# A decoder layer's attention: the projections written as one paced stream through DRAM

## The chip, the core and the metric

The kernel runs on one core of a Trainium2 chip. The core's engines work side by side, each on its own list of instructions in a fixed order: TensorE (PE in the profile, with its weight loads listed as PEld), VectorE (DVE), ScalarE (ACT), GpSimd (POOL) and SyncE (SP), which here issues nearly all DMAs. The metric is the device time of one execution in microseconds. Before the change it is 3108.72 us (median of three runs, 3105.47 to 3114.95).

## The reference

One decoder layer on 2048 tokens of width 1024, all in float32. The part that the change touches is the token mixer:

```
h = rms_norm(x, g_attn) * (1 + scale_a) + shift_a        # scale and shift from silu(c) @ w_ada
q_f, k_f, v_f, q_s, k_s, v_s, f_logit = split(h @ w_in)  # 8 + 8 heads of 64 columns
FoX:  s = q.k/8 + F[t] - F[s], causal;  softmax(s) @ v   # F = cumsum(log_sigmoid(f_logit + b))
SB:   z = q.k/8;  a[t,s] = sigmoid(z_ts) * prod_{s<j<t} (1 - sigmoid(z_tj)), s < t;  a @ v
x = x + gate_a * (concat(head_norm(o_fox), head_norm(o_sb)) @ w_out)
```

Behind it come a gated MLP with a short causal convolution (inner width 2752) and a final RMSNorm; the change does not touch them.

## The kernel before, in words

Every float32 product is made from two parts: `split` writes a rounded high part (a copy on ACT) and the remainder as a low part (a subtraction on DVE or POOL), and TensorE multiplies three of the four pairs (high with high, high with low, low with high) at the rate of the rounded type. Q.K takes two matmuls, because Q and K are laid out with high and low parts on 128 partitions.

Attention is cut into 32 units `(kind, p, tb)`: `kind` is `sb` (stick-breaking, first) or `fox`, `p` one of four pairs of heads, `tb` one of four blocks of 512 queries. The list runs over `tb` within `p` within `kind`, and unit 0 is `(sb, 0, 0)`. A unit with `tb` = 3 looks back over four blocks of keys, one with `tb` = 0 over one. Each unit has two bodies of work.

- **Projection** (`proj` and `finish_proj`, L368 and L284; `norm_proj` for the pair `(sb, 0)`, which also makes the normed input and stores it in the DRAM tiles `hs`). Eight input tiles `hp` are loaded from `hs` (10 buffers), 24 matmuls of 512 columns make q and 24 make k (both at L282, into the two PSUM banks `ps_pj`), and every second pair of heads also makes v for itself and the next pair (96 matmuls of 256 columns at L323, 264 for the first pair). q and k are split into tiles `q2` (2 buffers). From there four DMAs each copy them, from SBUF to SBUF, into the tiles `Q` (2 buffers) and `K` (5 buffers) that attention reads. v goes to a tile `V` (6 buffers); the second pair's goes through a tile `V` to the DRAM tile `vs` and is loaded from there later.
- **Attention** (`attend`, L492). A tile of logits is 128 queries by up to 512 keys: two matmuls (L405, L406) into `ps_qk`. For SB, ACT takes two sigmoids (L437, L438) and DVE runs the product as a scan (L443); for FoX, DVE adds the decay and finds the minimum (L472), and ACT takes the exponential (L476). Then TensorE transposes blocks of 128 (L415, into `ps_pt`), ACT and DVE split them into `at` (L419, L420), and TensorE multiplies with V (L424, 256 columns, into `ps_pv`).

The order of all this is set in two steps. In the source, `interleave` (L132) walks through the attention of unit i, and after each of its steps it takes steps of the projection of unit i+1, in proportion: 7, 12 or 19 projection steps over the unit's attention steps; what is left of that projection is written behind the last attention step. From the FoX unit 17 on, the same loop also takes four steps a unit of `late_mod`, which computes later modulation vectors from `w_ada` and folds a gate into `w_out` (its tiles are `hp` tiles too). Then a scheduler moves instructions: each engine gets its list by priority of the source's order, but what is ready sooner, by its own model of the buffers, is taken first. So the projection of unit i+1 is moved forward as far as its buffers let it: `Q` has two buffers, and the copy into the next one waits for the last logits of unit i-1.

A DMA whose buffer is not free yet waits at the head of SP's list, and everything behind it waits too.

## Time and profile before

| | |
|---|---|
| time of the profiled execution | 3105.93 us |
| its span, first to last instruction | 3103.7 us |
| granted TensorE clock, mean | 0.986 |
| startup and unit 0 (to its last product with V) | 105.6 us |
| units 1 to 31 | 105.6 to 1560.2 us |
| output projection, MLP and the rest | 1560.2 to 3103.7 us |
| DMA, mean over the span | 163 GB/s |

The boundaries of units used below are the starts of the last L424 matmul of each: a unit's window then holds its own attention, apart from a few logits of the next unit, and whatever projection work the scheduler put there. In a window's row, `(x771)` is the number of instructions that started in it. Matmuls overlap each other, so the busy time of PE is more than the time that their issue takes.

### The profile page before, as it was taken

Reading aid. Unit: us, or ns where it says so; the run is one execution under the profiler, and the core shown is the slowest. Engines: PE = TensorE matmul, PEld = TensorE weight load, DVE = VectorE, ACT = ScalarE, POOL = GpSimd, SP = SyncE. Lnnn points to the kernel's source line nnn. Section 1 sums busy time; section 2 is a strip of 40 time slices with the busy share of each in tenths; the row PEclk is TensorE's granted clock in tenths of the full one; section 3 lists DMA queues with packets and bytes.
Section 4 is the critical chain, followed back from the end, with each engine's and each line's share of the span. In section 5 each row is a group of like instructions: output and inputs, shape, how many; then the busy total and the mean of one; then the engine's idle time right before and its main releaser. Section 6 shows DMA issues by size and latency. Waiting matters only on the chain.

```text
span 3103.7 us, 45389 instructions
## 1 busy us (share of the span) xinstructions
PE 2955.7 (95%) x15934; PEld 2501.2 (81%) x15934; DVE 2071.3 (67%) x3206; ACT 1681.2 (54%) x3129; POOL 986.7 (32%) x1011
## 2 busy tenths in 40 slices
PE   6889999999999999999998899999899998999998
PEld 5788887878888888888877688888678887888887
DVE  6787777787857765567733687778977776254253
ACT  5676767677766665567634544444544443343332
POOL 1541321213131332341122344444444442332321
PEclk8999999999999999999999999999999999999999
DMA  9647654737264985694467522223222224565562
GB/s 270 225 136 265 194 166 118 250 99 211 73 191 159 318 271 174 191 319 125 138 200 225 190 79 85 82 83 88 85 82 82 82 82 147 183 203 166 184 201 87
DMA packets 301396, 504.85 MB, mean 163 GB/s; under 512 B 29712, under 2 KB 186128, under 8 KB 300144
## 3 DMA queue, kind: packets, MB, share of 16 engines
q1 hardware_dynamic: 289536, 489.32, 50.0%
q10 hardware_dynamic: 11632, 12.63, 1.2%
q8 instruction: 126, 2.06, 0.3%
q14 instruction: 102, 0.84, 0.1%
HBM read 356.81 MB, written 94.71 MB: 145 GB/s over the span
## 4 chain that ended last, share of the span: by engine, by line
PE 21%; DVE 10%; POOL 6%; DMA 6%; issue 5%; ACT 2%; SPq 0%; POOLq 0%; ACTq 0%; DVEq 0%
PE ps_o L984 8%; PE ps_t L984 4%; PE ps_bc L984 4%; DMA wuraw<-in_w_up_dram 3%; DVE wu L45 3%; PE ps_o L653 2%; PE ps_o L834 2%; DVE u L903 2%; POOL ws L822 2%; POOL wuraw L821 2%; POOL ws L820 1%; DVE u L924 1%; DVE u L902 1%; DMA r<-rstd 1%; PE ps_t L834 1%
## 5 line engine op out<-in xcount | busy, mean ns | idle before, releaser
L834 PE MATMUL ps_o<-oa,wu 128*128 128x512 f32 x2088 | 503.6, 392 | 13.1 <-DVE oa L45 6.8
L834 PEld LDWEIGHTS ps_o<-oa,wu 128*128 128x128 f32 x2088 | 390.9, 188 | 104.9 <-DVE oa L45 11.3
L420 DVE TENSOR_TENSOR at<-ps_pt,at 128x512 fp32r<-128x512 f32 (+1 forms) x576 | 362.6, 650 | 96.5 <-ACT at L419 94.5
L282 PE MATMUL ps_pj<-hp,w_qk 128*128 128x512 f32 x1512 | 414.0, 404 | 13.1 <-POOL hp L45 4.6
L443 DVE TENSOR_TENSOR_SCAN a<-r,a 128x512 f32<-128x512 f32 (+2 forms) x320 | 371.7, 1177 | 75.9 <-POOL a L440 41.1
L424 PE MATMUL ps_pv<-at,V 128*128 128x256 f32 x2304 | 397.9, 292 | 20.2 <-ACT at L419 9.4
L419 ACT ACTIVATE at<-ps_pt 128x512 fp32r<-128x512 f32 (+1 forms) x576 | 319.0, 578 | 132.8 <-PE ps_pt L415 106.3
L424 PEld LDWEIGHTS ps_pv<-at,V 128*128 128x128 f32 x2304 | 331.4, 190 | 58.9 <-DVE at L420 20.9
L282 PEld LDWEIGHTS ps_pj<-hp,w_qk 128*128 128x128 f32 x1512 | 274.9, 190 | 68.0 <-POOL hp L45 6.5
L45 DVE TENSOR_TENSOR wd<-wdraw,wd 128x1024 fp32r<-128x1024 f32 x88 | 112.4, 1277 | 261.2 <-ACT wd L44 261.1
L405 PE MATMUL ps_qk<-K,Q 128*128 128x512 f32 (+2 forms) x640 | 262.3, 411 | 10.5 <-ACT a L438 4.9
L984 PE MATMUL ps_o<-wd,g 128*128 128x512 f32 x1040 | 250.6, 390 | 8.8 <-ACT g L44 8.8
L45 POOL TENSOR_TENSOR g<-graw,g 128x512 fp32r<-128x512 f32 x84 | 141.1, 1682 | 326.8 <-ACT g L44 326.1
L834 PE MATMUL ps_t<-ob,wu 128*128 128x512 f32 x984 | 241.5, 390 | 0.0
L323 PE MATMUL ps_pj<-w_v,hp 128*128 128x256 f32 (+1 forms) x1536 | 235.8, 291 | 5.3 <-DVE w_v L45 1.8
L406 PE MATMUL ps_qk<-K,Q 128*128 128x512 f32 (+2 forms) x640 | 236.7, 371 | 0.0
L984 PEld LDWEIGHTS ps_o<-wd,g 128*128 128x128 f32 x1040 | 196.0, 189 | 49.9 <-ACT g L44 9.2
L44 ACT ACTIVATE wu<-wuraw 128x512 fp32r<-128x512 f32 x214 | 133.2, 627 | 186.3 <-PE ps_o L834 116.0
L323 PEld LDWEIGHTS ps_pj<-w_v,hp 128*128 128x128 f32 x1536 | 210.7, 193 | 14.2 <-DVE q L291 2.9
L834 PEld LDWEIGHTS ps_t<-ob,wu 128*128 128x128 f32 x984 | 184.7, 188 | 39.1 <-DVE y L886 0.4
L437 ACT ACTIVATE r<-ps_qk 128x512 f32<-128x512 f32 (+2 forms) x320 | 173.6, 543 | 78.2 <-PE ps_qk L406 75.5
L44 ACT ACTIVATE wd<-wdraw 128x1024 fp32r<-128x1024 f32 x88 | 93.1, 1058 | 206.8 <-PE ps_bc L984 193.0
(222 smaller groups left out, 5491.3 us busy)
## 6 DMA issues: line engine op xcount, KB each, us to landing
hp<-hs SPq DMA_DIRECT2D x224, 512.0 KB
wuraw<-in_w_up_dram SPq DMA_DIRECT2D x84, 512.0 KB
wdraw<-in_w_down_dram SPq DMA_DIRECT2D x84, 512.0 KB
Q<-q SPq DMA_DIRECT2D x128, 256.0 KB
g<-u SPq DMA_DIRECT2D x42, 512.0 KB
graw<-g SPq DMA_DIRECT2D x84, 256.0 KB
hs<-hp SPq DMA_DIRECT2D x32, 512.0 KB
K<-q SPq DMA_DIRECT2D x128, 128.0 KB
```

What stands on the lines that cost most here:

```text
L44: nc.scalar.activation(hi, src, AF.Copy)
L45: (lo_engine or nc.gpsimd).tensor_sub(lo, src, f(hi))
L282: nc.tensor.matmul(acc, w[kt][:, a, n], h[:, bb], start=kt == 0 and i == 0, stop=kt == KT - 1 and i == 2)
L323: nc.tensor.matmul(av[:, t * width:(t + 1) * width], hts[kt][:, a, tok], w[1][kt][:, bb, 0:width], start=kt == 0 and m == 0, stop=kt == KT ...
L405: nc.tensor.matmul(b[:, :cw], Q[:, hl, 0, qcols], K[:, hl, :cw], start=True, stop=False)
L406: nc.tensor.matmul(b[:, :cw], Q[:, hl, 1, qcols], K[:, hl, :cw], start=False, stop=True)
L419: nc.scalar.activation(at[:, 0, lo:], b[:, lo:], AF.Copy)
L420: nc.vector.tensor_sub(at[:, 1, lo:], b[:, lo:], f(at[:, 0, lo:]))
L424: nc.tensor.matmul(o[:, 0:2 * P], V[kt // 4][:, kt % 4, hl, :], rhs, start=first and kk == 0 and w == 0, stop=last and kk == 1 and w == 1)
L443: nc.vector.tensor_tensor_scan(rev, r[:, 0:need][:, ::-1], rev, 0.0 if right[qi] is None else right[qi][:, 0:1], ALU.mult, ALU.add)
L834: nc.tensor.matmul(b, w[:, p, j], o[:, q], start=first and i == 0, stop=last and i == 2, skip_group_check=True)
L984: nc.tensor.matmul(banks[t][n], g[:, a, t * P:(t + 1) * P], w[:, b, n * TB:(n + 1) * TB], start=k == 0 and i == 0, stop=k == NKD - 1 and i ...
```

## The change

Four things are written differently; no arithmetic is added or left out.

1. **The projections of units 1 to 31 are one generator**, `project()`, called `ahead`. It is not tied to the next unit any more. `pace(i)` gives, for each attention step of unit i, how many projection steps are to be written by then: the larger of two lines. The first brings the next unit's projection to its end at 0.8 of this unit's steps. The second, from unit 3 on, spreads all remaining projection steps over units 3 to 29 in proportion to a weight of the units' attention, 10 + 16 tb, times 1.4 for SB.
2. **A bound on how far the scheduler moves them.** From unit 3 on, each projection step is written inside `issue_after(...)`: its TensorE instructions stand behind the second logits matmul that is the thirteenth to last written (`LAG` = 12). That is an order on TensorE's list alone, not a wait.
3. **Q, K and V go through DRAM**, but for the pair `(sb, 0)`, whose Q and K, and whose own V, are copied as before. Otherwise `q2` and `k2` are written to a DRAM tile of their own for each unit, both V's to `vs`, and `load_unit` reads them into `Q`, `K` and `V` when the attention of the unit before is under way. The V's that are to be stored are made in `q2` buffers. `V` has 5 buffers in place of 6.
4. `Fb` (the FoX decay, broadcast) has 10 buffers in place of 8.

```diff
-    def finish_proj(kind, p, tb, aq, w, hts, res, ak=None):
+    def staged():
+        return sl_.tile([P, 2, TB], F32R, name="q2", bufs=2)
+    def load_unit(kind, p, tb, res):
+        if (kind, p) == ("sb", 0):
+            return
+        Q, K, V = unit_tiles()
+        src = qs.pop((kind, p, tb))
+        for h in range(2):
+            rows = slice(h * HD, (h + 1) * HD)
+            for r in range(2):
+                half = slice(r * HD, (r + 1) * HD)
+                nc.sync.dma_start(f(Q[half, h]), src[rows, 0])
+                nc.sync.dma_start(f(K[half, h]), src[rows, 1, r])
+        nc.sync.dma_start(f(V), vs[kind][p][tb])
+        res.append((Q, K, V))
+    def finish_proj(kind, p, tb, aq, w, hts, ak=None):
...
+        if direct:
+            for h in range(2):
+                for r in range(2):
+                    nc.sync.dma_start(f(Q[r * HD:(r + 1) * HD, h]), f(q2[h * HD:(h + 1) * HD]))
+        else:
+            q_ = qs[kind, p, tb] = dram.tile([P, 2, 2, TB], F32, name=f"qk_{kind}{p}_{tb}", bufs=1)
+            nc.sync.dma_start(q_[:, 0], f(q2))
...
-            nc.sync.dma_start(spill, f(V1))
+            for e in range(direct, 2):
+                nc.sync.dma_start(vs[kind][p + e][tb], f(Vs[e]))
...
+    def pace(i):
+        n = attend_steps(units[i])
+        due = sum(proj_steps(u) for u in units[:i + 2])
+        total = sum(proj_steps(u) for u in units)
+        done = sum(weight(u) for u in units[START:i])
+        span = sum(weight(u) for u in units[START:STOP])
+        base = sum(proj_steps(u) for u in units[:START + 1])
+        first = projected[0]
+        for m in range(1, n + 1):
+            yield max(first + (due - first) * min(1.0, m / (0.8 * n)),
+                      base + (total - base) * (done + weight(units[i]) * m / n) / span if i >= START else 0)
+    LAG = 12
+    LATE, PER = 17, 4
+    START, STOP = 3, 30
...
+        def follow(m):
+            while projected[0] < goals[min(m, n - 1)]:
+                with tc.issue_after(marks[max(0, len(marks) - 1 - LAG)]) if i >= START else nullcontext():
+                    if next(ahead, 1) is not None:
+                        break
+            if nxt and projected[1] > i + 1 and loaded_units[0] == i + 1:
+                loaded_units[0] += 1
+                load_unit(*nxt, results[nxt[:2]])
-        interleave(attend(kind, p, tb, results[kind, p], Fbs), n,
-                   [(nxt and proj_gen(nxt), steps, True),
-                    (lm if kind == "fox" and (p, tb) != (0, 0) else None, 4, False), (tail, 12, True)])
+        interleave(attend(kind, p, tb, results[kind, p], Fbs), n, [(lm if i >= LATE else None, PER, False), (tail, 12, True)], follow)
+        while nxt and loaded_units[0] == i + 1:
+            next(ahead, None)
+            follow(n)
```

What this makes of the engines' lists is shown at three places. Line numbers of the new kernel are larger: L284 and L355 are its projection matmuls, L442 and L443 its logits, L452 its transposes, L461 its products with V.

**The middle of unit 11, `(sb, 2, 3)`, on PE.** Before, in rows from the middle of a stretch:

```order
L415 MATMUL ps_pt<-edge,a 128x128 x4
L405 MATMUL ps_qk<-K,Q 128x384
L406 MATMUL ps_qk<-K,Q 128x384
L424 MATMUL ps_pv<-at,V 128x256 x3
L415 MATMUL ps_pt<-edge,a 128x128 x2
L405 MATMUL ps_qk<-K,Q 128x512
L406 MATMUL ps_qk<-K,Q 128x512
L424 MATMUL ps_pv<-at,V 128x256
L415 MATMUL ps_pt<-edge,a 128x128 x2
L424 MATMUL ps_pv<-at,V 128x256 x4
L415 MATMUL ps_pt<-edge,a 128x128 x4
L405 MATMUL ps_qk<-K,Q 128x512
```

And now, in the same unit:

```order
L442 MATMUL ps_qk<-K,Q 128x512
L443 MATMUL ps_qk<-K,Q 128x512
L284 MATMUL ps_pj<-hp,w_qk 128x512
L452 MATMUL ps_pt<-edge,a 128x128 x2
L442 MATMUL ps_qk<-K,Q 128x512
L443 MATMUL ps_qk<-K,Q 128x512
L284 MATMUL ps_pj<-hp,w_qk 128x512 x5
L452 MATMUL ps_pt<-edge,a 128x128 x2
L284 MATMUL ps_pj<-hp,w_qk 128x512 x6
L452 MATMUL ps_pt<-edge,a 128x128 x4
L284 MATMUL ps_pj<-hp,w_qk 128x512
L461 MATMUL ps_pv<-at,V 128x256 x8
```

Projection matmuls now stand between a unit's logits and its transposes, where before there was attention alone.

**The seam between SB and FoX (units 15 and 16), on PE and on ACT.** Before, PE, from the last products with V of unit 15 to the first transposes of FoX (`ps_pt<-edge,p`):

```order
L282 MATMUL ps_pj<-hp,w_qk 128x512 x3
L424 MATMUL ps_pv<-at,V 128x256 x3
L282 MATMUL ps_pj<-hp,w_qk 128x512
L323 MATMUL ps_pj<-w_v,hp 128x256 x34
L509 MATMUL ps_pt<-headsel,sq 128x2 x2
L323 MATMUL ps_pj<-w_v,hp 128x256 x44
L405 MATMUL ps_qk<-K,Q 128x256
L406 MATMUL ps_qk<-K,Q 128x256
L323 MATMUL ps_pj<-w_v,hp 128x256
L405 MATMUL ps_qk<-K,Q 128x256
L406 MATMUL ps_qk<-K,Q 128x256
L415 MATMUL ps_pt<-edge,p 128x128
```

Now, PE:

```order
L461 MATMUL ps_pv<-at,V 128x256 x11
L547 MATMUL ps_pt<-headsel,sq 128x2 x2
L284 MATMUL ps_pj<-hp,w_qk 128x512 x12
L442 MATMUL ps_qk<-K,Q 128x256
L443 MATMUL ps_qk<-K,Q 128x256
L452 MATMUL ps_pt<-edge,p 128x128
```

ACT just behind, before (L575 is `late_mod`'s product of a loaded `w_ada` tile, L476 the exponential of unit 16):

```order
L476 ACTIVATE p_10439,ls_10368<-p_10439,mn_10443 128x128
L476 ACTIVATE p_10460,ls_10368<-p_10460,mn_10464 128x256
L419 ACTIVATE at_10414<-ps_pt_10413 128x384
L44 ACTIVATE V_10936<-ps_pj_11252 128x4x64
L575 ACTIVATE hp_11031<-hp_11031,cs_263 128x512 x2
L44 ACTIVATE V_11133<-ps_pj_11252 128x4x64
L419 ACTIVATE at_10472<-ps_pt_10471 128x384
L530 ACTIVATE o2_10435<-ps_pv_10369 64x256
L476 ACTIVATE p_10507,ls_10368<-p_10507,mn_10511 128x384
```

ACT now, at the last exponentials of unit 16 and the first of unit 17 (L513, the same operation; L613 is `late_mod`'s):

```order
L513 ACTIVATE p_11186,ls_10987<-p_11186,mn_11190 128x384
L456 ACTIVATE at_11171<-ps_pt_11170 128x384
L513 ACTIVATE p_11197,ls_10987<-p_11197,mn_11201 128x512
L568 ACTIVATE o2_11079<-ps_pv_11038 64x256
L456 ACTIVATE at_11209<-ps_pt_11208 128x512
L613 ACTIVATE hp_11523<-hp_11523,cs_279 128x512
L513 ACTIVATE p_11251,ls_11249<-p_11251,mn_11260 128x640
```

78 of PE's projection matmuls have left the seam and 12 others stand there; `late_mod`'s first ACT products have moved from among the first exponentials of FoX to behind the eighth.

**SP's list around the load of Q for unit 12, `(sb, 3, 0)`.** Before, where Q and K come straight from `q2`:

```order
L304 DMA K_7853<-q2_7856 64x512 x4
L308 DMA V_8320<-vs_sb1_1_213 128x1024
L373 DMA hp_8488<-hs2_2_78 128x1024
L373 DMA hp_8493<-hs2_3_79 128x1024
L373 DMA hp_8548<-hs2_4_80 128x1024
L373 DMA hp_8553<-hs2_5_81 128x1024
L373 DMA hp_8598<-hs2_6_82 128x1024
L373 DMA hp_8603<-hs2_7_83 128x1024
L373 DMA hp_8860<-hs3_0_84 128x1024
L373 DMA hp_8865<-hs3_1_85 128x1024
L294 DMA Q_7852<-q2_7855 64x1024 x4
L373 DMA hp_8938<-hs3_2_86 128x1024
```

And now (L322 and L336 write q and k to DRAM, L304 loads Q, L410 loads inputs):

```order
L336 DMA qk_sb3_1_7566<-q2_7695 128x1024
L322 DMA qk_sb3_2_7889<-q2_7886 128x1024
L304 DMA Q_7637<-qk_sb3_0_7245 64x1024 x4
L410 DMA hp_8099<-hs3_2_86 128x1024
L410 DMA hp_8104<-hs3_3_87 128x1024
L410 DMA hp_8121<-hs3_4_88 128x1024
L410 DMA hp_8126<-hs3_5_89 128x1024
L410 DMA hp_8159<-hs3_6_90 128x1024
L410 DMA hp_8164<-hs3_7_91 128x1024
L410 DMA hp_8454<-hs0_0_60 128x1024
L410 DMA hp_8459<-hs0_1_61 128x1024
L336 DMA qk_sb3_2_7889<-q2_8008 128x1024
```

The load of Q for unit 12 now stands among the writes of units 13 and 14, with input loads and such a write behind it, where before it came from `q2` itself with input loads behind it.

102 lines of the change are left out of this document (67 added, 35 removed).

## The prediction

> **What bounds the kernel now.** I read the page first, then the stretches of the attention stage unit by unit, then which instructions of projection ran in each, then the waits of SP and ACT.
>
> ```profile
> PE 2955.7 (95%) x15934; PEld 2501.2 (81%) x15934; DVE 2071.3 (67%) x3206; ACT 1681.2 (54%) x3129; POOL 986.7 (32%) x1011
> ```
>
> PE looks full, but its matmuls overlap, so its idle time must be found another way. The stretches are units 4 to 6, 7, 8 to 10, 11, 12 to 14 and 15 (so every second one is a unit with tb = 3), with ten microseconds out of unit 11 between; then FoX with projections, FoX pair 3 without, and a stretch of the MLP.
>
> ```profile
> core 0: us, PE busy (x) PEld busy (x) DVE busy (x) ACT busy (x) POOL busy (x), PEclk, DMA share, GB/s
> 330.10:449.20 119.10, 114.97 (x771) 103.18 (x770) 90.62 (x121) 82.66 (x190) 33.23 (x48) 1.00 0.58 174
> 449.20:521.80 72.60, 65.61 (x419) 56.23 (x418) 55.17 (x72) 51.38 (x111) 11.93 (x16) 0.95 0.27 75
> 521.80:643.00 121.20, 117.99 (x754) 104.76 (x752) 87.25 (x118) 80.52 (x179) 31.16 (x41) 1.00 0.72 232
> 643.00:700.80 57.80, 53.34 (x337) 43.91 (x336) 50.91 (x66) 45.60 (x99) 7.43 (x11) 1.00 0.33 104
> 660.00:670.00 10.00, 9.18 (x57) 7.28 (x57) 9.87 (x12) 9.02 (x19) 1.45 (x2) 1.00 0.00 0
> 700.80:814.50 113.70, 109.63 (x735) 98.00 (x733) 90.60 (x123) 84.03 (x196) 27.03 (x45) 1.00 0.50 148
> 814.50:876.80 62.30, 58.56 (x371) 48.87 (x370) 50.97 (x67) 45.62 (x96) 5.36 (x8) 1.00 0.32 99
> 876.80:1423.80 547.00, 531.43 (x3498) 477.22 (x3497) 345.28 (x878) 346.76 (x672) 187.94 (x240) 0.99 0.72 233
> 1423.80:1560.20 136.40, 131.01 (x854) 114.10 (x853) 104.52 (x272) 95.50 (x173) 23.82 (x43) 0.99 0.41 129
> 1862.00:2017.00 155.00, 154.57 (x679) 126.84 (x678) 119.19 (x139) 68.55 (x98) 63.81 (x64) 1.00 0.28 84
> ```
>
> In the middle of unit 11, DVE is busy 9.87 of 10 us and ACT 9.02, and no DMA moves: DVE's scans set the pace there and PE waits for them. Now the same stretches for the projection matmuls alone, of 512 columns (L282), then of 256 (L323):
>
> ```profile
> 330.10:449.20 119.10, 37.06 (x136) 24.49 (x136) 1.00 0.58 174
> 449.20:521.80 72.60, 9.66 (x32) 5.58 (x32) 0.95 0.27 75
> 521.80:643.00 121.20, 51.35 (x187) 33.28 (x187) 1.00 0.72 232
> 643.00:700.80 57.80, 7.29 (x29) 5.37 (x29) 1.00 0.33 104
> 700.80:814.50 113.70, 32.75 (x120) 21.79 (x120) 1.00 0.50 148
> 814.50:876.80 62.30, 11.29 (x47) 8.60 (x47) 1.00 0.32 99
> 876.80:1423.80 547.00, 168.58 (x625) 114.61 (x625) 0.99 0.72 233
> ```
> ```profile
> 330.10:449.20 119.10, 30.00 (x192) 26.27 (x192) 1.00 0.58 174
> 449.20:521.80 72.60, 12.93 (x73) 11.57 (x73) 0.95 0.27 75
> 521.80:643.00 121.20, 19.26 (x119) 16.43 (x119) 1.00 0.72 232
> 643.00:700.80 57.80, 0.00 (x0) 0.00 (x0) 1.00 0.33 104
> 700.80:814.50 113.70, 24.99 (x165) 22.13 (x165) 1.00 0.50 148
> 814.50:876.80 62.30, 4.95 (x27) 3.95 (x27) 1.00 0.32 99
> 876.80:1423.80 547.00, 87.35 (x576) 78.24 (x576) 0.99 0.72 233
> ```
>
> The tb = 3 units of SB hold the fewest projections per unit of attention, and unit 11 almost none. To say what PE loses I need the time at which it issues. The MLP stretch gives 155.0/679 = 0.228 us for 512 columns; runs of equal matmuls in the timeline give (5.44-0.28)/43 = 0.120 for 256 columns and (0.60-0.28)/3 = 0.107 for a transpose:
>
> ```profile
> 881.57 5.44 PE L323 MATMUL ps_pj<-w_v,hp 128*128 128x256 f32 x44
> 870.30 0.60 PE L415 MATMUL ps_pt<-edge,a 128*128 128x128 f32 x4
> ```
>
> (0.28 is about the length of the last one; the single transpose quoted further down took 0.27.) The loops fix the attention of a unit with tb = 3 at 64 logits matmuls (52 of 512, 4 of 384, 8 of 256 columns: 13.5 us), 120 products with V (14.4), 116 transposes (12.4) and 8 small ones (0.9), in all 41.2 us; tb = 0 to 2 together need 58.1 in the same way (96 logits 18.6, 168 products 20.2, 156 transposes 16.7, 24 small 2.6). With their projections, units 4 to 6 need 58.1 + 136 x 0.228 + 192 x 0.120 = 112.1 of 119.1 us, units 8 to 10 115.0 of 121.2, units 12 to 14 105.3 of 113.7: together 332.4 of 354.0, or 93.9%. Units 7, 11 and 15 need 57.3 of 72.6, 47.8 of 57.8 and 55.1 of 62.3: 160.2 of 192.7, or 83.1%. FoX with projections needs 3 x 99.3 + 625 x 0.228 + 576 x 0.120 = 509.5 of 547.0, 93.1%. FoX pair 3, with no projection, needs 99.3 and these
>
> ```profile
> L653 PE MATMUL ps_bc<-wo,mix 128*128 128x512 f32 x96 | 24.9, 400 | 1.5 <-DVE p L657 1.5
> ```
>
> 96 x 0.228 = 21.9, so 121.2 of 136.4, 88.9%. SB attention alone starves PE; FoX much less so.
>
> How the gap is measured matters for the sum. By PE's busy column the three units stand at 177.5/192.7 = 92.1% and the mixed ones at 342.6/354.0 = 96.8%, and the sum below would give -9.3 us, no more than the measure. [...]
>
> **The change part by part.** *Pacing, in units 7, 11 and 15.* In the new list these hold 87, 96 and 60 projection matmuls of 512 columns and 96, 61 and 104 of 256, where they held 108 and 100 in all. So 135 x 0.228 + 161 x 0.120 = 50.1 us of PE's work moves in. DVE does not forbid it: it is busy 50.91 us in unit 11 and 55.17 in unit 7, which had 105 projections, while PE would then need about 70. At the rate of the mixed units the three take (160.2 + 50.1)/0.939 = 224.0 us, 31.3 more. The same 50.1 us leave other units, mostly FoX and units 0 to 3, where they took 50.1/0.939 = 53.4. Net: -22.1. If the three units reach only 90%, it is -12; at 95%, -25.
>
> *FoX with fewer projections.* Units 21 and 25 keep 24 and 38 of them. Their attention needs 19.4 us each; at 88.9% in place of 93.1% that costs 38.8 x (1/0.889 - 1/0.931) = +2.0. Nothing (if what is left is enough) to +4 bounds it.
>
> *The seam.* FoX cannot start before its decay tiles have landed. PE bridges this wait with the projection of v:
>
> ```profile
> 877.16 4.21 PE L323 MATMUL ps_pj<-w_v,hp 128*128 128x256 f32 x34
> 887.44 0.27 PE L415 MATMUL ps_pt<-edge,p 128*128 128x128 f32 x1
> 894.59 1.33 ACT L575 ACTIVATE hp<-hp,cs 128x512 f32<-128x512 f32 x2 [4.22 <-DMA hp<-in_w_ada_dram]
> ```
>
> Between 877.16 and the first FoX transpose at 887.44 run 78 x 0.120 = 9.4 us of it; the new list has 12 x 0.228 = 2.7 there. If the wait is as long, PE idles 6.7 us more. Against it, ACT stood 4.22 us in front of a `w_ada` tile, with exponentials behind; that product now stands behind them. I take +6.7 - 4.2 = +2.5, between -4.2 and +6.7.
>
> *Q, K and V through DRAM.* 28 units are spilled (all but the four of the first pair): 1 MB more is written for each (the loads replace copies of the same size), and 12 of them write and read one more V of 0.5 MB. That is 40 MB over the 1094 us of units 4 to 27, 37 GB/s; from the DMA columns (0.50 for 152 GB/s is their mean over units 4 to 15, by the rows above) that is 0.12 of the DMA engines, on 0.50 in SB and 0.72 in FoX. It is hidden while they are below full and while nothing waits for a landing. At the starts of pairs they are full already (units 4 and 20):
>
> ```profile
> 330.10:350.90 20.80, 19.52 (x112) 16.12 (x111) 15.53 (x22) 16.21 (x43) 8.87 (x16) 1.00 0.96 291
> 1053.60:1068.90 15.30, 14.96 (x96) 12.70 (x95) 12.87 (x38) 12.46 (x31) 6.18 (x12) 1.00 1.03 386
> ```
>
> There K and V of the three later units of the pair can now be loaded at once with Q, 4 MB or 10 us at 386 GB/s, at seven starts: +73 if none of it were covered. But PE is busy 19.52 of 20.80 and 14.96 of 15.30 us there, full DMA engines or not. For a landing I have the same kind of round trip in the values of SB, 512 KB out and in again, and the queue's own waits:
>
> ```profile
> SPq L362 <- DMA vd<-xt: 23.4, 4, 8.6
> POOL xt L363 <- DMA xt<-vd: 18.4, 3, 8.9
> SPq L294 <- PE ps_qk L406: 104.5, 12, 34.6
> ACT q L44 <- DMA Q<-q: 24.3, 12, 4.5
> ACT q L290 <- DMA K<-q: 11.0, 7, 3.4
> ```
>
> 5.9 us to land and 6.1 to come back, 12 us. By `pace`, from the end of unit 3 on at least one unit beyond the next is finished, two to four in most places, so the write is over long before; the load is issued when a Q buffer comes free, as the copy was, and has the current unit's length to land. Cover gone, it would be up to 12 us a unit. I take 0. The last two rows may gain a little: ACT waited 35.3 us for `q2` while its copies waited for Q, and a write to DRAM does not. But 28 V's are now made in the same two buffers. From -11 (a third of those waits on the path) to +11; taken at 0. The 80 more DMA issues on SP, one V buffer fewer and two more for `Fb` cost nothing that a row shows, while SP has the long waits above as slack.
>
> Sum: -22.1 + 2.0 + 2.5 = -17.6 on the profiled execution's 3105.9, so 3088.3. That execution lies 2.8 below the median of the runs; on the median I expect 3091.
>
> **The rivals.** *A: as above.* 3091.
>
> *B: a finer mix helps everywhere.* The new list has one stretch in units 4 to 15 in which PE would work over 6 us without a projection, against five before. If the whole of units 4 to 27, which needs 332.4 + 160.2 + 509.5 = 1002.1 of 1093.7 us, comes to the 94.9% of the best row (units 8 to 10), it takes 1056.0, and with the seam the sum is -37.7 + 2.5: 3074. For it: DVE and ACT are near 75% in the mixed rows. Against it: in FoX the longer projection-free pieces do not get fewer.
>
> *C: filler does not help the three units.* Unit 7 had the most projections of the three (105) and the lowest rate, 78.9%. If the chain of scan, transposes and copies sets 83.1% whatever stands between, the three take (160.2 + 50.1)/0.831 = 253.1, 60.4 more, against 53.4 saved: +7.0, with the other terms +11.5: 3120. Against it: unit 7's projections were bunched at both ends, and units 4 to 6 have the same chain.
>
> *D, the slower side: SP's order.* A load of Q waits for logits at the head of SP's list: 12 such waits, 8.7 us each, one of 34.6. Behind it now stand the writes that free `q2`, and ACT, which fills `q2`, waits in order with the exponentials behind it. If each of the 28 spilled units loses the 2.0 us (24.3/12) that ACT lost at one such wait, it is +56: 3147. Above 0.63 us a unit (17.6/28) the gain is gone. For it: `q2` has still two buffers and serves V too. Against it: before, the copy to Q waited itself with its `q2` held; now only the queue's order ties them. [...]
>
> **How the numbers follow.** A measurement of this kernel cannot tell less than 0.3%, 9.3 us, from no change: 3099.4 to 3118.0. I give A 0.48, B 0.24, C 0.08, D 0.20. A's own range is 3079 to 3103 (its terms at their ends, not all at once). Faster: most of A (0.42) and B: 0.66. Within 0.3%: the rest of A, half of C, and a D that stops near break-even: 0.14. Slower: 0.20. The range reaches from B with a little more to spare, 3055, to half of D's price, 3135.
>
> **What the new profile would show.** Right: units 7, 11 and 15 longer, near 75 us each, with weight loads at 85% or more, and DMA share no longer near 0 in unit 11; DVE there below 80%; FoX shorter. Seam: PE idle some 6 us before the first FoX transpose. Rival D: waits of ACT for DMA writes of `q2` over 60 us in all, or PE waits for Q or K. C: the three units beyond 82 us each. I am wrong if the landing of Q, K and V, or the input tiles, come late at the starts of pairs, where a burst of loads is new.

## The result, and the profile after

The changed kernel takes 3109.65 us (median of 12 runs, 3102.14 to 3116.41), the kernel before, on the same chip, 3106.17 (12 runs, 3101.5 to 3114.95). The ratio is 1.0007 with a 95% interval of 0.9993 to 1.002: no change that can be told. The prediction was 3091, 0.6% below, so a clear gain was forecast and none came. The profiled execution took 3108.77 us with a span of 3106.8, 3.1 more than the span before.

First the page's engine shares; they are the old ones to 1%, and tell nothing.

```profile
PE 2957.1 (95%) x15934; PEld 2510.1 (81%) x15934; DVE 2063.9 (66%) x3206; ACT 1682.7 (54%) x3129; POOL 977.3 (31%) x1011
```

Then the stretches of the changed kernel, cut as before at the last product with V of a unit: all of units 4 to 15, units 7, 11 and 15 alone, the seam (unit 16), units 17 to 27, and FoX pair 3.

```profile
core 0: us, PE busy (x) PEld busy (x) DVE busy (x) ACT busy (x) POOL busy (x), PEclk, DMA share, GB/s
337.10:879.80 542.70, 535.79 (x3604) 482.70 (x3604) 431.74 (x574) 395.71 (x877) 113.91 (x172) 1.00 0.62 204
447.70:522.00 74.30, 73.88 (x493) 66.42 (x491) 56.56 (x69) 52.20 (x113) 17.40 (x21) 1.00 0.59 194
628.60:702.90 74.30, 72.45 (x468) 63.60 (x468) 60.76 (x76) 57.41 (x128) 21.61 (x28) 1.00 0.68 218
811.20:879.80 68.60, 67.53 (x467) 61.54 (x466) 56.44 (x73) 51.87 (x110) 10.43 (x16) 1.00 0.54 174
879.80:923.40 43.60, 30.92 (x132) 23.59 (x130) 14.51 (x49) 18.46 (x43) 15.17 (x22) 0.79 0.99 285
923.40:1424.30 500.90, 475.96 (x3097) 423.61 (x3097) 322.48 (x815) 317.78 (x602) 158.09 (x203) 0.98 0.75 246
1424.30:1563.50 139.20, 133.33 (x873) 115.93 (x871) 105.49 (x275) 99.10 (x179) 31.19 (x51) 1.00 0.41 137
```

The kernel before, in the same view, for the two FoX stretches that the prediction had as one:

```profile
876.80:915.00 38.20, 33.46 (x220) 29.95 (x219) 16.35 (x51) 21.09 (x51) 19.02 (x26) 0.91 0.89 293
915.00:1423.80 508.80, 497.98 (x3281) 447.28 (x3280) 328.93 (x827) 325.68 (x622) 168.92 (x214) 1.00 0.71 229
```

Units 7, 11 and 15 took 72.6, 57.8 and 62.3 us and take 74.3, 74.3 and 68.6 with 50 us more of projections in them. FoX did not get shorter although it lost that work: from the end of unit 15 to the last product with V it is 683.4 us before and 683.7 now.

I count, for each stretch, the issue time that PE lost: the window less the time that its matmuls need one behind the other. Each matmul record of the trace is taken at a fixed price near the median spacing of back-to-back ones: 0.227 us for 512 columns, 0.175 for 384, 0.118 for 256, 0.107 for a transpose, 0.06 for a small one. These prices are a little lower than the prediction's, so the sums are higher (63.8 in SB before, where its count gives 54.1); the differences between kernels are nearly the same. All kernels in us, each from one profiled execution; medians and ratios are against runs of the kernel before on the same chip:

| kernel | median | ratio, 95% | units 4-15 | 16 | 17-27 | 28-31 |
|---|---|---|---|---|---|---|
| before | 3106.17 | | 63.8 | 8.7 | 32.9 | 18.4 |
| changed | 3109.65 | 1.0007 [0.9993, 1.002] | 28.6 | 23.3 | 56.3 | 17.2 |
| e1 first limit of pace only, no bound | 3108.90 | 1.0014 [1.0005, 1.0024] | 51.6 | 13.3 | 42.3 | 17.4 |
| e2 no bound | 3108.26 | 1.0010 [0.9997, 1.0022] | 50.2 | 17.2 | 43.4 | 17.9 |
| e3 bound in SB only | 3086.32 | 0.9939 [0.9925, 0.9953] | 27.1 | 18.1 | 44.2 | 15.7 |
| e4 even weight | 3097.29 | 0.9966 [0.9954, 0.9978] | 35.0 | 10.7 | 51.0 | 22.4 |
| e5 early decay | 3098.83 | 0.9976 [0.9965, 0.9986] | 28.4 | 9.2 | 55.5 | 20.6 |
| e6 late stage's modulation in SB | 3128.37 | 1.0068 [1.0053, 1.0083] | 90.1 | 15.6 | 23.1 | 17.6 |
| e6b the same, on the kernel before | 3138.30 | 1.0096 [1.0076, 1.0116] | 91.6 | 5.9 | 32.0 | 21.2 |
| e7 before, with the writes | 3106.93 | 0.9996 [0.9986, 1.0007] | 61.0 | 10.9 | 32.2 | 20.1 |
| e9 = e3 + e5 | 3088.06 | 0.9937 [0.9922, 0.9951] | 25.9 | 11.8 | 46.7 | 17.3 |
| e12 = e5, bound 32 in FoX | 3086.09 | 0.9934 [0.9920, 0.9947] | 28.1 | 11.0 | 47.3 | 16.0 |
| e13 = e12, modulation from unit 20, denser | 3103.81 | 0.9988 [0.9977, 0.9999] | 27.5 | 6.5 | 72.1 | 18.7 |
| e14 = e12, even weight | 3082.50 | 0.9917 [0.9901, 0.9932] | 31.7 | 7.9 | 44.8 | 15.9 |
| e15 changed, modulation thinner | 3105.90 | 0.9998 [0.9986, 1.0010] | 28.7 | 19.6 | 44.2 | 35.5 |
| e16 = e14, modulation thinner | 3089.55 | 0.9940 [0.9926, 0.9954] | 29.7 | 6.6 | 47.3 | 17.7 |
| e17 = e16, from unit 14 | 3081.93 | 0.9920 [0.9903, 0.9938] | 37.4 | 7.1 | 47.7 | 12.0 |

How far one profiled execution can be trusted: e7 has nearly the same PE list as the kernel before, and its stretches differ from it by 0.7 to 2.8 us, so differences of that size are not told apart below. The profiled executions of e2, e4, e7, e15 and e17 took 3114.30, 3105.03, 3111.81, 3115.11 and 3087.38 us, 5 to 9 above their medians; in e2, e7, e15 and e17 4 to 7 of that lie behind attention (1548.8, 1550.0, 1547.7 and 1547.3 us, against 1543.3 in the changed kernel). Those of e9 and e16 lie 6.9 and 5.2 below theirs.

Changed against before, SB gives 35.2 us, the seam takes 14.6 back and units 17 to 27 take 23.4; units 0 to 3 (+1.5), pair 3 (-1.2) and all that follows (-0.2) hardly move. That sums to +2.9 beside the 3.1 of the spans. The gain was made, and FoX spent it.

**The seam.** The timeline of the changed kernel, the rows on PE, POOL, DVE and SP that carry it (start, length, then in brackets the idle time ahead and who ended it):

```profile
881.49 1.61 SPq L410 DMA_DIRECT2D hp<-hs  x2
885.27 1.65 PE L284 MATMUL ps_pj<-hp,w_qk 128*128 128x512 f32 x3 [2.86 <-DMA hp<-hs]
885.30 7.17 SPq L781 DMA_DIRECT2D Fb<-fs  x8
891.83 0.64 POOL L507 TENSOR_SCALAR_AFFINE_SELECT Fd<-Fb 128x128 f32<-128x128 f32 x2 [10.08 <-DMA Fb<-fs]
904.02 3.11 POOL L611 TENSOR_SCALAR hp<-hp,cs 128x512 f32<-128x512 f32 x2 [8.62 <-DMA hp<-in_w_ada_dram]
907.08 1.47 POOL L507 TENSOR_SCALAR_AFFINE_SELECT Fd<-Fb 128x384 f32<-128x384 f32 x3
907.62 0.56 DVE L509 CUSTOM_DVE_ANT_0 p<-ps_qk,Fd 128x384 f32<-128x384 f32 x1 [7.69 <-POOL Fd L507]
908.24 0.79 PE L442 MATMUL ps_qk<-K,Q 128*128 128x512 f32 x1 [4.76 <-DVE mn L509]
```

and the same place before:

```profile
881.13 4.92 SPq L696 DMA_DIRECT2D Fb<-fs  x8
884.97 0.65 POOL L470 TENSOR_SCALAR_AFFINE_SELECT Fd<-Fb 128x128 f32<-128x128 f32 x2 [6.25 <-DMA Fb<-fs]
```

The decay is used 8.2 us after SB's last unit before, and 12.0 us after it now. SP has loads of input tiles in front of the eight decay loads; these are issued 5.5 us after the last unit in place of 4.3, and the first mask follows 6.5 us behind the first of them in place of 3.8, with the DMA engines at 0.99 in the row of unit 16 against 0.89. PE, which had 78 value products here, has a few projections whose own tiles come late too. Then POOL stands 8.62 us in front of a `w_ada` row with the next decay mask behind it; DVE waits for the mask and PE for DVE. In the row of unit 16 the granted clock is 0.79, so the clock is worth up to 9.2 of its 43.6 us, against 3.4 of 38.2 at 0.91 before. The trace has the clock at 0.50 from 884.2 to 894.4 us, from 908.1 to 911.4 and from 918.3 on. The first of these falls begins within the gap of 2.86 us, with another of 1.68 just ahead of it, the second at the end of the gap of 4.76, the third at the end of one of 1.98 before 918.33. At 0.50 the six projection matmuls from 889.88 take 2.72 us; at 1.00 the twelve from 899.66 take 2.74.

**Units 17 to 27.** The projections there, of 512 columns (L282, now L284) and of 256 (L323, now L355), in the kernel before and then in the changed one:

```profile
915.00:1423.80 508.80, 158.58 (x594) 1.00 0.71 229
915.00:1423.80 508.80, 74.94 (x480) 1.00 0.71 229
```
```profile
923.40:1424.30 500.90, 134.91 (x507) 0.98 0.75 246
923.40:1424.30 500.90, 54.22 (x384) 0.98 0.75 246
```

That is 87 x 0.227 + 96 x 0.118 = 31.1 us less of them. What stands beside them is the modulation of the later stage (`late_mod` and `fold_out`: rows of `w_ada` and `w_out` loaded, scaled by ACT or DVE and added up by POOL). Its groups in this stretch, before and after:

```profile
L575 ACT ACTIVATE hp<-hp,cs 128x512 f32<-128x512 f32 x50 | 33.2, 714 | 22.6 <-DMA hp<-in_w_ada_dram 21.0 <-issue 1.6
L542 DVE SCALAR_TENSOR_TENSOR hp<-hp,cols 128x512 f32<-128x512 f32 x16 | 11.8, 776 | 0.0
```
```profile
L613 ACT ACTIVATE hp<-hp,cs 128x512 f32<-128x512 f32 x48 | 31.9, 716 | 31.4 <-DMA hp<-in_w_ada_dram 27.4 <-issue 4.0
L580 DVE SCALAR_TENSOR_TENSOR hp<-hp,cols 128x512 f32<-128x512 f32 x16 | 11.6, 761 | 5.6 <-DMA hp<-in_w_out_dram 5.6
```

The work is nearly the same and the waits are longer. One of them in the changed kernel's timeline:

```profile
1086.53 1.41 DVE L580 SCALAR_TENSOR_TENSOR hp<-hp,cols 128x512 f32<-128x512 f32 x2 [3.38 <-DMA hp<-in_w_out_dram]
1088.46 0.68 DVE L509 CUSTOM_DVE_ANT_0 p<-ps_qk,Fb 128x512 f32<-128x512 f32 x1
1088.60 0.81 PE L452 MATMUL ps_pt<-edge,p 128*128 128x128 f32 x4 [2.80 <-DVE at L457]
```

DVE takes its list in order: a `w_out` row comes late (3.38 us), the split (L457) and the logits behind it wait, and PE with them (2.80 us), since no projection stands there. The clock falls to one half 0.4 us behind this gap of 2.80 us and right at the end of another, of 2.29, at 1102.63; behind gaps of 2.25 us before 1168.62 and 2.03 before 1370.64 it stays at 1.00. Both stretches in rows:

```profile
1090.00:1100.00 10.00, 10.00 (x55) 8.87 (x53) 8.79 (x22) 7.29 (x16) 5.18 (x7) 0.71 0.94 310
1100.00:1110.00 10.00, 7.71 (x47) 6.80 (x47) 9.14 (x22) 8.07 (x16) 5.62 (x6) 0.83 1.02 355
```

In units 17 to 27 of the changed kernel the trace has the clock at one half from 923.4 to 925.1, 1089.0 to 1095.8, 1102.6 to 1106.0 and 1297.2 to 1300.6 us (the first is the end of the stretch from 918.3, the last comes behind a gap of 2.42), which is worth up to 7.7 us; in the kernel before it is there once, for 3.4 us from 1219.9, behind a gap of 2.72, worth up to 1.7. So up to some 6 of the 23.4 us are the lower clock at PE's waits, and not the waits themselves.

### The profile page after: what moved, and what is told of

It reads as the page before. It is cut to its first block, busy times and chain, and to the rows that moved or that the text cites. A ratio compares the mean times of both kernels' runs of the same rounds, so it can differ in the third digit from the quotient of the medians.

```text
span 3106.8 us, 45436 instructions
## 1 busy us (share of the span) xinstructions
PE 2957.1 (95%) x15934; PEld 2510.1 (81%) x15934; DVE 2063.9 (66%) x3206; ACT 1682.7 (54%) x3129; POOL 977.3 (31%) x1011
## 4 chain that ended last, share of the span: by engine, by line
PE 54%; DMA 15%; DVE 11%; POOL 7%; issue 7%; ACT 5%; SPq 1%; POOLq 0%; DVEq 0%; ACTq 0%
PE ps_pj L284 8%; PE ps_o L1077 8%; PE ps_pv L461 7%; PE ps_pt L452 6%; PE ps_pj L355 5%; PE ps_t L1077 4%; PE ps_bc L1077 4%; PE ps_qk L442 3%; PE ps_o L927 3%; PE ps_qk L443 3%; DMA wuraw<-in_w_up_dram 3%; DVE wu L45 3%; DMA hp<-in_w_ada_dram 2%; DVE u L996 2%; PE ps_o L736 2%
## 5 line engine op out<-in xcount | busy, mean ns | idle before, releaser
L284 PE MATMUL ps_pj<-hp,w_qk 128*128 128x512 f32 x1512 | 417.0, 405 | 21.9 <-DMA hp<-hs 16.0
L457 DVE TENSOR_TENSOR at<-ps_pt,at 128x512 fp32r<-128x512 f32 (+1 forms) x576 | 364.9, 651 | 107.1 <-ACT at L456 104.5
L461 PE MATMUL ps_pv<-at,V 128*128 128x256 f32 x2304 | 408.2, 295 | 13.8 <-DVE at L457 5.6
L480 DVE TENSOR_TENSOR_SCAN a<-r,a 128x512 f32<-128x512 f32 (+2 forms) x320 | 363.1, 1153 | 82.8 <-POOL a L477 41.6
L461 PEld LDWEIGHTS ps_pv<-at,V 128*128 128x128 f32 x2304 | 336.7, 192 | 48.4 <-DVE at L457 14.6
L284 PEld LDWEIGHTS ps_pj<-hp,w_qk 128*128 128x128 f32 x1512 | 275.2, 191 | 79.0 <-DMA hp<-hs 20.8
L442 PE MATMUL ps_qk<-K,Q 128*128 128x512 f32 (+2 forms) x640 | 267.5, 419 | 20.4 <-DVE mn L509 11.7
L443 PE MATMUL ps_qk<-K,Q 128*128 128x512 f32 (+2 forms) x640 | 238.7, 374 | 0.0
L355 PE MATMUL ps_pj<-w_v,hp 128*128 128x256 f32 (+1 forms) x1536 | 232.0, 289 | 3.6 <-DVE w_v L45 1.4
L355 PEld LDWEIGHTS ps_pj<-w_v,hp 128*128 128x128 f32 x1536 | 209.2, 191 | 13.6 <-DVE q L315 2.4
```

What stands on the lines that cost most here:

```text
L284: nc.tensor.matmul(acc, w[kt][:, a, n], h[:, bb], start=kt == 0 and i == 0, stop=kt == KT - 1 and i == 2)
L355: nc.tensor.matmul(av[:, t * width:(t + 1) * width], hts[kt][:, a, tok], w[1][kt][:, bb, 0:width], start=kt == 0 and m == 0, stop=kt == KT ...
L442: nc.tensor.matmul(b[:, :cw], Q[:, hl, 0, qcols], K[:, hl, :cw], start=True, stop=False)
L443: marks.append(nc.tensor.matmul(b[:, :cw], Q[:, hl, 1, qcols], K[:, hl, :cw], start=False, stop=True).ins)
L457: nc.vector.tensor_sub(at[:, 1, lo:], b[:, lo:], f(at[:, 0, lo:]))
L461: nc.tensor.matmul(o[:, 0:2 * P], V[kt // 4][:, kt % 4, hl, :], rhs, start=first and kk == 0 and w == 0, stop=last and kk == 1 and w == 1)
```

## The experiments

The theory: SB's gain is real, and FoX lost as much because it had lived on the projections that were taken away: at the seam, and wherever the late stage's modulation holds up an engine. The rivals: the trip through DRAM costs by itself; the bound of twelve logits holds PE up; FoX lacks filler whatever stands beside it.

**e1: only the first limit of pace, no bound.**

```
-    START, STOP = 3, 30
+    START, STOP = 32, 33
```

> The stream goes through DRAM, but only the first of the two limits of pace is left (a unit ahead by the time 80% of the present one is issued), and no logit holds a projection back. Units 7 and 11 then hold about 35 and 31 us of projections (31 and 29 in the changed kernel, 16 and 7 before), but unit 15 holds 12 and units 16 to 18 none. Theory (SB gains, FoX gives it back where it has too little filler): SB gains 15 to 30 us, units 16 to 18 lose 20 or more, together 3105 to 3125. Rival (the trip through DRAM costs by itself, whatever the pacing): units 7 and 11 gain nothing, and the whole is at 3125 or more. Rival (the second limit of pace is what helps SB): units 7, 11, 15 are at 83% as before and the time is 3106 or more.

Measured 3108.90; SB loses 51.6 us, between the changed kernel's 28.6 and the 63.8 before. Units 7 and 11 are full, but units 8 and 15 lose 9.1 and 13.8: the filler stands bunched. SB gained 12.2, less than the theory said; the whole lies where it said. The trip through DRAM alone is not at 3125 or more. The last rival holds for unit 15, not for 7 and 11 (2.4 and 1.4 us lost).

**e2: no bound anywhere; e3: the bound only up to unit 15.**

```
-                with tc.issue_after(marks[max(0, len(marks) - 1 - LAG)]) if i >= START else nullcontext():
+                with nullcontext():                                                                             # e2
+                with tc.issue_after(marks[max(0, len(marks) - 1 - LAG)]) if START <= i < 16 else nullcontext():  # e3
```

> The changed kernel without the twelve-logit bound anywhere; pacing by both limits. Theory (FoX lost for want of filler at its start and for late transfers, the bound only settles where the filler stands): SB keeps most of its gain of 35 us (units 7 and 11 have 35 and 31 us of filler, unit 15 has 35), units 16 to 18 hold no projection and lose 15 to 30 us more than in the changed kernel: 3115 to 3140. Rival (the bound holds PE up in FoX, so that without it the lost 37 us come back): 3080 or less.

> The bound only up to unit 15. SB as in the changed kernel, instruction for instruction; units 16 to 18 hold no projection (8.9, 11.6 and 16.3 us in the changed kernel), unit 27 none (17.7). Theory: the same SB, FoX worse by 15 to 30 us: 3120 to 3140. Rival (the bound holds PE up in FoX): 3080 or less. A middle result, within 5 us of 3110, would say that FoX loses by late transfers and not by the place of the filler.

Without the bound (3108.26) SB loses 50.2 us in place of 28.6: the bound is worth 21.6 us there, not only a matter of place, as the theory had it; the whole is below its 3115 as well. Beside e1 (51.6) it also shows that the second limit of pace alone gives SB nothing. And units 16 to 18, which hold no projection at all here, lose 21.7 us, less than the 28.0 of the changed kernel and not 15 to 30 more. With the bound in SB alone the kernel takes 3086.32, 0.68% less than the changed one by the two ratios, and the theory's 3120 to 3140 is clearly wrong. (Its statement on units 16 to 18 was wrong too: they hold 10.9, 13.6 and 16.3 us of projections in this kernel; only that unit 27 holds none was right.) So the bound of twelve costs in FoX: 12.1 us in units 17 to 27 and 5.2 at the seam. This is the stretch of units 17 to 27:

```profile
920.50:1408.30 487.80, 470.88 (x3092) 420.62 (x3090) 324.50 (x815) 317.86 (x606) 163.17 (x208) 0.99 0.77 254
```

It holds 161.0 us of projections (161.7 in the changed kernel; sums of projections are at the prediction's 0.228 and 0.120 us), yet loses 44.2 and not 56.3. But 3080 or less, the rival's number if the bound were all of it, was not reached.

**e5: the two first decay tiles a unit earlier, in tiles of their own.**

```
+        if u == ("sb", 3, 2):
+            for h in range(2):
+                decay.append(sb.tile([P, TB], F32, name=f"decay{h}"))
+                nc.sync.dma_start(decay[h], fs[h:h + 1, 0:TB].to_broadcast([P, TB]))
...
-            Fbs = [[sx.tile([P, TB], F32, name="Fb", bufs=10) for _ in range(NTB)] for _ in range(2)]
+            Fbs = [[decay[h] if decay and t == 0 else sx.tile([P, TB], F32, name="Fb", bufs=8) for t in range(NTB)] for h in range(2)]
```

> The changed kernel with the two decay tiles of the first FoX unit loaded one unit earlier, into two tiles of their own, so that FoX need not wait for them at the seam; everything else as it was. Theory (the wait for the decay costs the seam its 14.6 us): unit 16 falls from 43.6 us to 30 to 34, half rate there goes, and the whole is 9 to 14 us shorter than the changed kernel: 3096 to 3101. Rival (something else is late next at the same place, the w_ada tiles or the input tiles): unit 16 stays above 38 and the whole is within 4 us of 3110.

Measured 3098.83, 0.31% less than the changed kernel, as the theory said. The window of unit 16 and its first masks:

```profile
880.60:908.30 27.70, 23.36 (x123) 19.22 (x122) 13.82 (x45) 14.29 (x36) 9.23 (x17) 0.88 0.96 294
```
```profile
882.47 0.64 POOL L507 TENSOR_SCALAR_AFFINE_SELECT Fd<-decay 128x128 f32<-128x128 f32 x2
885.78 1.65 PE L284 MATMUL ps_pj<-hp,w_qk 128*128 128x512 f32 x3 [2.61 <-DMA hp<-hs]
```

43.6 us became 27.7 with nearly the same projections (36 matmuls in place of 39), and 14.1 us of lost time went; the input tiles are late as before. The clock is at 0.88, so it did not go back to full: its worth fell from 9.2 to 3.3 us at most, so more than half of what went is the wait itself. The late decay, and with it the lower clock (0.79 against 0.88), is what the seam cost.

**e9: both.** The bound as in e3, the decay as in e5.

> Both edits that gained, together: the twelve-logit bound only up to unit 15, and the two decay tiles of FoX's first unit loaded a unit earlier. Theory (the bound costs 23 us in FoX, the late decay 11 us at the seam, two places): 3075 to 3080. Rival (both shorten the same seam, and half of the one is in the other): 3083 to 3090.

3088.06: no better than e3 alone, and in the rival's range. In the profile the seam does gain (11.8 against 18.1), but units 17 to 27 lose 2.5 more and the part behind attention took 2.7 more (1542.2 us against 1539.5), both no more than two executions differ by; the medians do not show a gain.

**e12: early decay, and a bound of 32 in FoX.**

```
-... marks[max(0, len(marks) - 1 - LAG)]
+... marks[max(0, len(marks) - 1 - (LAG if i < 16 else 32))]
```

> Early decay as before, and in FoX a bound of 32 logits behind the attention done, where it was 12; SB keeps 12. Theory (what costs in FoX is that projections may not run ahead by more than 12 logits, while FoX units with small tb have few logits): most of the gain of leaving the bound away, 3076 to 3085. Rival (any bound costs there, since it ties PE's order to one point): 3095 to 3100, as with the bound of 12 and the early decay.

3086.09: one us above the theory's range and far below the rival's. Units 17 to 27 lose 47.3, as without any bound (46.7 in e9), against 55.5 in e5. Not that there is a bound but its tightness costs in FoX.

**e6: the later stage's modulation in SB; e6b: the same edit on the kernel before.**

```
-    LATE, PER = 17, 4                                          # e6, on the changed kernel
+    LATE, PER = 4, 5
...
-                    (lm if kind == "fox" and (p, tb) != (0, 0) else None, 4, False), (tail, 12, True)])   # e6b, before
+                    (lm if i >= 4 else None, 5, False), (tail, 12, True)])
```

> The changed kernel with the modulation of the later stage (the rows of w_ada, w_out and the work on them) begun in unit 4 in place of unit 17, so that FoX holds none of it; the bound and the decay as in the changed kernel. Theory (part of what FoX gave back is waits of ACT, POOL and DVE for these rows, 49 us in the changed kernel, with exponentials and decay work queued behind): FoX shorter by 8 to 15 us and SB longer by less than 5: 3097 to 3105. Rival (SB, which is limited by DVE, takes as much as FoX gains, or these waits are off the path): 3107 or more.

> The kernel before with the modulation of the later stage begun in unit 4 in place of unit 17 (five steps a unit), so that FoX holds none of it: the same edit that took the issue time lost in units 17 to 27 of the changed kernel from 56.3 to 23.1 us. Theory (in the kernel before FoX had more projections and they covered these stalls): units 17 to 27 lose 24 to 31 us in place of 32.9. Rival (the modulation costs FoX the same in both kernels, and the changed one lost its time elsewhere): they lose 12 or less. In both cases SB loses 25 to 65 us more and the whole is at 3125 to 3165.

As times both are losses (3128.37 and 3138.30): SB loses 61.5 and 27.8 us more, so the rival of e6 was right on the whole. But they price the modulation in FoX. Units 4 to 15, then units 17 to 27, of e6 and then of e6b:

```profile
338.90:949.70 610.80, 572.15 (x3659) 507.76 (x3658) 474.04 (x600) 433.78 (x940) 229.29 (x241) 0.96 0.71 235
984.40:1449.00 464.60, 458.67 (x3072) 415.97 (x3071) 309.48 (x798) 282.97 (x542) 72.22 (x137) 0.99 0.61 196
```
```profile
340.30:921.20 580.90, 538.29 (x3428) 468.99 (x3427) 468.59 (x588) 422.34 (x922) 225.28 (x232) 0.98 0.60 193
960.10:1461.60 501.50, 491.02 (x3240) 439.88 (x3239) 311.68 (x810) 283.16 (x549) 73.07 (x139) 1.00 0.57 173
```

ACT does 60 instructions and 34.8 us less in units 17 to 27 of e6 than in the changed kernel (317.78 to 282.97), and 42.5 less in e6b than before. In the changed kernel the lost time falls by 33.2 us, from 56.3 to 23.1, with the same projections (161.0 against 161.7 us); in the kernel before by 0.9, from 32.9 to 32.0. The same work was free in the kernel before and costs 33 us in the changed one. No other edit moves FoX as much. PE's waits for input tiles go with it, first the changed kernel, then e6:

```profile
L284 PE MATMUL ps_pj<-hp,w_qk 128*128 128x512 f32 x507 | 134.9, 399 | 8.8 <-DMA hp<-hs 8.8
```
```profile
L284 PE MATMUL ps_pj<-hp,w_qk 128*128 128x512 f32 x504 | 128.2, 394 | 0.0
```

The modulation's work on the engines, its loads and its `hp` tiles all leave together, and these runs do not separate them. Nor do they say that the missing projections make the difference: e6 has the bound of twelve and no more projections than the changed kernel and loses less than the kernel before; and in SB the same edit costs the changed kernel more than the kernel before (61.5 against 27.8) although more projections stand there (229 us in e6, 197 in e6b). The bound and the modulation are also not two prices to be added: 12.1 and 33.2 are more than the 23.4 that were lost. The 32.0 of e6b lies just above the theory's 24 to 31 and far from the rival's 12.

**e7: the kernel before with the writes alone.** After the copies of `q2` and `k2` of the 28 later units, both are also written to a DRAM tile that nothing reads:

```
+        if (kind, p) != ("sb", 0):
+            nc.sync.dma_start(qx[kind, p, tb][:, 0], f(q2))
...
+            nc.sync.dma_start(qx[kind, p, tb][:, 1], f(k2))
```

> The kernel before, unchanged but for 56 more writes: q2 and k2 of the 28 later units also go to DRAM (28 MB), and nothing reads them. It prices the traffic and the queue entries without the new order. Theory (hidden, beside DMA at 0.50 in SB and 0.72 in FoX): within 5 us of the kernel before. Rival (the traffic makes other transfers late, and that is what FoX lost): 10 to 30 us more than the kernel before, most of it in units 16 to 27.

3106.93, ratio 0.9996, and no stretch moves by more than 2.8 us: 28 MB of writes and 56 DMA entries are hidden.

**e13: e12 with the modulation from unit 20, six steps a unit (`LATE, PER = 20, 6`).**

> The version with the bound of 32 in FoX and the early decay (3086 us), with the modulation of the later stage begun in unit 20 in place of 17, six steps a unit in place of four. Theory (its rows and the work on them collide with the first FoX units, where the decay, the weights of the next pair and the input tiles come too): units 16 to 20 lose 18 to 22 us in place of 30.8, the later ones 0 to 5 more: 3076 to 3083. Rival (the same work costs the same wherever in FoX it stands, or more where it is denser): 3085 to 3100.

3103.81: the rival, and beyond it. Units 16 to 20 lose 34.0 us and not 18 to 22, and units 17 to 27 lose 72.1 in place of 47.3. The same work, denser, costs 24.8 us more; 20.9 of them lie in units 19 to 27, where it stands.

**e15: the changed kernel with the modulation at three steps a unit (`LATE, PER = 17, 3`).**

> The changed kernel with one number changed: the modulation of the later stage advances three steps a unit in place of four, from unit 17 as before, so that it reaches into the last pair, which has no projections. Theory (its stalls reach PE where they stand too dense for the filler that FoX has left): units 17 to 27 lose 40 to 48 us in place of 56.3, the last pair up to 4 more, the whole 3097 to 3104. Rival (the amount of this work counts and not its spread, or FoX lacks filler whatever stands beside it): 3107 to 3113.

3105.90, not told apart from the changed kernel. Units 17 to 27 do lose 44.2 in place of 56.3, as the theory said, but pair 3, which has hardly any projections, loses 35.5 in place of 17.2, and not up to 4 more:

```profile
919.10:1407.70 488.60, 471.35 (x3087) 420.00 (x3086) 325.32 (x817) 307.37 (x584) 132.16 (x183) 0.99 0.74 239
1407.70:1565.70 158.00, 141.73 (x885) 123.01 (x884) 108.39 (x274) 113.36 (x201) 61.36 (x74) 0.95 0.50 166
```

ACT's busy time moves by 10.4 us from the one stretch and by 14.3 to the other, and the lost time goes with it. Where the modulation stands without any filler, PE loses 18.3 us more.

**e4: SB weighted 1.0 in place of 1.4 in the pace.**

```
-        return 1.4 * tri(u[2]) if u[0] == "sb" else tri(u[2])
+        return tri(u[2])
```

> The changed kernel with SB units weighted 1.0 in place of 1.4 and nothing else: the bound of twelve stays in FoX, the decay is late as before. About 24 us of projections move from SB to FoX. If FoX lost for want of projections: units 17 to 27 lose 35 to 45 us in place of 56.3 and the whole is at 3092 to 3102. If the bound kept those it had from the places where they were needed: 50 us or more are still lost there and the whole is within 5 us of 3110.

3097.29, in the range for want of projections. But the place is another: 12.6 of the gain is at the seam, where 72 of the value products stand again and the decay is not late as expected: its first mask comes 6.0 us after SB's last unit, in place of 12.0. Units 17 to 27, with 598 and 480 projections in place of 507 and 384 (32 us more, and as many as before the change), still lose 51.0, which is the answer for the bound. So at the seam this run does not tell the projections from the decay; behind it, having the projections back is worth 5.3 of 56.3 us.

**e14: e4's weight on e12. e16 and e17: that with the modulation at three steps a unit, from unit 17 and from unit 14.**

> The same version (3086 us) with SB units weighted 1.0 in place of 1.4 in the pace, so that some 20 to 30 us of projections move from SB back to FoX. Theory (SB starves without them, FoX with the loose bound does not): units 4 to 15 lose 10 to 20 us more than 28.1, FoX gains under 10: 3089 to 3100. Rival (FoX still lacks filler as much as SB does): 3080 to 3087.

> The fastest version so far (even weight, bound of 32 in FoX, early decay: 3082.5 us) with three steps a unit of that modulation in place of four. Theory: units 17 to 27 lose 34 to 40 us in place of 44.8: 3072 to 3079. Rival: 3081 to 3087, since with more projections in FoX nothing is left to gain, or since the thinner work now meets the last pair, which has no filler at all.

> As the one before, with the modulation begun in unit 14 in place of 17, at three steps a unit. Theory (SB's last two units have slack for six steps, since DVE and not ACT limits them): SB loses up to 4 us more, FoX a little less: 3072 to 3080. Rival (SB cannot take any of it, as when all of it stood there and SB lost 62 us more): 3084 to 3095.

e14 takes 3082.50, in the rival's range: SB gives up 23.4 us of projections and loses only 3.6 more. But units 17 to 27 lose 2.5 us less than in e12, no more than two executions differ by, so the rival's reason, that FoX lacks filler, is not borne out. e16 (3089.55) is slower than e14, above its theory's range and above its rival's 3087 too. e17 (3081.93) is as fast as e14, between its theory and its rival, and not by the way that was named: SB loses 5.7 us more than in e14, units 17 to 27 2.9 more, and pair 3 3.9 less. e14 and e17 are the fastest: 0.8% below the kernel before, each with an interval that ends below 0.994.

What the theory keeps: the seam, and that the modulation's stalls reach PE. What it loses: that the amount of projections decides it in units 17 to 27. Without the bound of twelve they lose 43.4 us with 131 us of projections (e2), 42.3 with 166 (e1), 44.8 with 192 (e14, a bound of 32).

What stays open: e14 has as many projections in units 17 to 27 as the kernel before (588 and 480, against 594 and 480), and a bound of 32, and still loses 44.8 us there against 32.9. Every version through DRAM that keeps the modulation there loses 9 us or more over the kernel before. PE's own waits for input tiles are part of it (7.1 us in units 17 to 27 of e14, 8.8 in the changed kernel, 2.9 before), but the rest was not traced. The reads of Q, K and V from DRAM were not tried by themselves either; in the changed kernel they take the place of copies of the same size.

## Why the prediction was wrong

**Pacing in units 7, 11 and 15: right in kind, too small.** It said 224.0 us for the three at 93.9%; they take 217.2, at 96.8% by the prediction's prices (210.3 us of need). The nine other SB units went from 93.9% to 96.4% too. Against -22.1 with ends at -12 and -25, SB measured -35.2. DVE stayed at 76 to 82% there and weight loads at 86 to 90%. In SB alone, rival B's finer mix did happen. e2 shows which part of the change made it: without the bound 21.6 of these 35.2 us are gone; e1, with neither the bound nor the second limit of pace, keeps 12.2.

**FoX with fewer projections: this step failed.** It said +2.0, between 0 and +4; units 17 to 27 lost 23.4 more. It priced the amount of projections left in two thin units, at pair 3's rate of 88.9%, and put two other things at nothing. The first is their place: the bound of twelve, which pays in SB, costs 12.1 us there (e3), and a bound of 32 does not (e12). The second is what the late stage's modulation costs in the new order: 33.2 us, against 0.9 in the kernel before (e6, e6b); pair 3, which gave the rate, has hardly any of it. The two overlap: with the modulation gone, the kernel with the bound of twelve loses only 23.1 us there. I read that as the bound keeping projections behind logits while the stalls come at loads, but no run shows it by itself. The amount, the one thing that the step did price, was worth little, as it said: 5.3 us under the bound of twelve (e4) and 2.5 under 32 (e14). Why the versions without the bound of twelve still lose 42 to 48 us there, where 32.9 were lost before, is not shown.

**The seam: failed in size.** It said +2.5, between -4.2 and +6.7; it is +14.6. It saw that the value products had bridged the wait, but took the wait to be as long as before; the decay was used 3.8 us later, 1.2 of them since SP issued its loads later, behind input tiles, and 2.7 since the first mask came later behind its load. The 4.2 us that ACT was to gain at `w_ada` came back as 8.62 us on POOL. And the clock's part, up to 9.2 us, was not priced. e5 shows the place: 14.1 us gone with the decay early. What the missing bridge cost by itself no run shows: in e4 the value products are back, but the decay comes sooner too.

**Q, K and V through DRAM at 0: held** for the writes of Q and K, as far as e7 goes; the reads and the V's were not tried. Rival D did not come about. It needed some 60 us of ACT waiting for writes of `q2`; the longest such row in the changed kernel's waits is this one:

```profile
ACT q L314 <- DMA vs_sb<-q: 4.3, 3, 2.9
```

Rival C fell as well (units at 97% and not 83%). The case that came, SB gaining more than forecast and FoX spending it all, was in no rival; that the sum came out at no change is chance, SB 13 us better than forecast against 33 us worse at the seam and behind it. The text's last line had only late tiles at the starts of pairs as a danger; input tiles did come late, for 8.8 us in units 17 to 27, but mostly in the middle of pairs.

## What to carry to other kernels

Before moving independent work between stages, price the stage that gives it with everything that shares its engines, buffers and queue there, and not by a quieter stretch without them; here the quiet stretch gave +2.0 and the stage lost 23.4. Give back the moved work in one run before calling its absence the cause: here that returned 5.3 us of 23.4. Make a bound on run-ahead a number for each stage: twelve logits were worth 21.6 us in SB and cost 12.1 in FoX, and 32 in FoX cost nothing that could be told. At a change of stage, look first at what the next stage must load before it can start, and load that earlier, before spending filler on bridging it.

## What was not expected of the hardware

Work that waits for loads did not cost here what it took: some 43 us of ACT's time (33.2 us in the row of L575, 9.9 in the split of the scaled `w_out`) cost PE 0.9 us in the kernel before, 33.2 in the changed one, and, from e12 to e13, 24.8 more when it was packed into fewer units. And the clock, of which I had not thought at all, fell at PE gaps of 2.29, 2.80 and 4.76 us: it was worth up to 9.2 of 43.6 us at the seam, at a granted 0.79, and up to 7.7 in units 17 to 27.
